# Five local edits and one order table in a fused two-block kernel on Trainium2

## The chip, the core and the metric

The kernel runs on one core of one Trainium2 chip. The metric is the device time of one execution in microseconds (us). A comparison is made between medians of runs of the two kernels on the same chip. A core has five engines that run their own instruction queues and meet at semaphores: TensorE (PE, matmuls), VectorE (DVE), ScalarE (ACT), GpSimd (POOL) and SyncE (SP, which here only issues DMAs).

## The reference, cut to what matters

The input is one sequence of 512 tokens with 1024 channels. A first block adds a mixer (a bidirectional state-space branch and a windowed attention, gated and joined) and an MLP; a second block has its own mixers, a cross attention to a memory and a second MLP. The state-space branch has 8 groups of 4 heads:

```python
def rmsnorm(x, g):
    y = xf * lax.rsqrt(jnp.mean(xf * xf, axis=-1, keepdims=True) + EPS)
    return y * g
...
def ssd_branch(z, xbc, dt_raw, conv_w, conv_b, dt_bias, a_log, d_skip, norm_w, w_out):
    xbc = jax.nn.silu(depthwise_conv(xbc, conv_w, conv_b))
    xs, bs, cs = split_cols(xbc, (D_INNER, G * N, G * N))
    dt = jax.nn.softplus(dt_raw + dt_bias);  a = -jnp.exp(a_log)
    y = ssd_scan(xs, dt[0], a[0], bs, cs) + flip(ssd_scan(flip(xs), ...)) + xs * d_skip
    y = gated_rmsnorm(y, z, norm_w)          # silu(z), then a norm within each group
    return y @ w_out
...
x = x + rmsnorm(mixed, post_mix_norm);  h = rmsnorm(x, pre_mlp_norm)
f = jnp.square(jax.nn.relu(h @ w_mlp_in)) @ w_mlp_out
x = x + rmsnorm(f, post_mlp_norm)
```

The second block's mixer projects the normed x to, among others, three latents of 256, 128 and 64 columns, each with an rms norm of its own. The last MLP of the kernel is multiplied by a scheme that replaces eight block products by seven (products n = 0 to 6, sums of blocks p1, c11, c12, c21, c22).

## The kernel before, in words

All products are in fp32 made of two halves: an operand is split into a high part (hh, whi, ua_h, by ACT) and the remainder (hl, wlo, ua_l, by DVE), and three matmuls add up one product: lines L286 to L288 with 512 moving columns, L304 to L306 with 256. Weights come in tiles of 128x1024 (raw); L140 casts one to whi on ACT and L141 takes the rest, wlo, on DVE. Tiles in PSUM are eight banks, named after their users (psg, pse, psc, pso, psy, pst).

The program is written in source order with Python lists of steps; a scheduling layer then fixes the order on each engine. `issue_after(x)` holds instructions back until x has been issued, `keep_in_program_order` keeps one in its place. On an engine instructions run strictly in that order.

*Start.* x comes in four tiles of 128 tokens. For each, ACT squares one half and DVE the other, two short DVE instructions form the mean, POOL takes the power -0.5, and DVE and ACT scale one half each (L417, L418) before PE transposes. The bias dtb and alog are loaded 4 bytes per partition on SP's queue, behind the weights of bc0; dtb is first used by dt_evac (L486), alog by L490. gpre (L400) is the first norm's gain, transposed by PE.

*State-space groups.* `Group` is one of 8 groups; a group takes some 52 us. A loop runs a list of steps, GSEQ, which mixes the second half of group g with the preparation of group g+1: z0 to z3 are the projections of z for the current group, f0 to f7 the projections and convolutions of the next group's channels (psg evacuated by L591 to cbuf and L592, four taps on DVE at L594, silu at L595), xt0 and xt1 the transposes of its two tiles of x (L600, copied by L601), st, w and y the states, weights and outputs (L667 with xw of L664, L697, L705), norm the group's norm (squares L724, the power on POOL at L343, scaling of sz at L729), u0 and u1 the transposes of the normed result (L734, split by L337 and L338 into ua_h and ua_l), e0 to e3 the exponents of the decay (PE L685, Exp L687 on ACT, masking L688 and sum L692 on POOL), cb the product of C and B (L656). rows loads rh and lh for the exponents on POOL's queue. silu and Exp need different tables on ACT, so a change between them costs an ACT_TABLE_LOAD. In the fifth group the f steps also carry half of the output projection.

*After a block's output.* `post_norm` works in eight tiles k: pn and the sum into xT (L1027, L1028), the split into hh and hl (L337, L338), and the squares of the new x for the next norm, by `SumSq`: a square on ACT (L1008) and an add into ssq on POOL (L1009). It runs twice: in front of the first block's MLP (PE L1045 to L1047) and in front of the second block's mixer (`project`, PE L1248 to L1250). `token_sums` sums ssq over channels with a product by ones on PE (L349).

*Latents.* `inv_rms` takes mean and power of one latent's four columns (L342, L343), three times.

*Last quarter.* Products n = 0 to 6 run over two row halves i. What is ready is copied and added into the blocks (L1804, `add`, L1784) by the table LAST, and DONE says which is stored after which product. Each of the products has a bank of PSUM for each half.

Of the kernel before, what the change touches and what calls it, by code (L numbers as in the profile page):

```python
# [16 lines left out]
P = 128  # L17
# [11 lines left out]
GSEQ = """  # L29
z0 w0 xt1 st0 z1 w1 z2 z3 st1 silu st2 y0 f0 f1 y1 rows f2 f3 w2 e0 y2 e1 w3 f4 f5 bt y3 norm f6 e2 xt0 f7 u0 u1 cb e3  # L30
"""
# [53 lines left out]
def body(ctx, tc, a, out, dbg=None):  # L85
# [318 lines left out]
    for t in range(NT):  # L404
        for i in range(2):
            xs = xn[:, t, i * 512 : i * 512 + 512]
            junk = sb("cacc", bufs=3)
            if i == 0:
                A.activation(junk, xs, AF.Square, accum_out=ss0[:, t, i : i + 1])
            else:  # L410
                V.tensor_tensor_reduce(out=junk, in0=xs, in1=xs, scale=1.0, scalar=0.0, op0=ALU.mult, op1=ALU.add,
                                       accum_out=ss0[:, t, i : i + 1])
        rt = r0[:, t : t + 1]
        V.tensor_tensor(out=rt, in0=ss0[:, t, 0:1], in1=ss0[:, t, 1:2], op=ALU.add)
        V.tensor_scalar(out=rt, in0=rt, scalar1=1.0 / D, scalar2=EPS, op0=ALU.mult, op1=ALU.add)
        last = tc.keep_in_program_order(G.tensor_tensor(out=rt, in0=rt, in1=mhalf[:, 0:1], op=ALU.pow))
        V.tensor_scalar(out=xn[:, t, 0:512], in0=xn[:, t, 0:512], scalar1=rt, scalar2=None, op0=ALU.mult)  # L417
        A.activation(xn[:, t, 512:1024], xn[:, t, 512:1024], AF.Copy, scale=rt)  # L418
        for k in range(KT):
# [42 lines left out]

    dtb = const([P, 1], "dtb")
    alog = const([P, 1], "alog")
    with tc.issue_after(unit_of["bc", 0].last.ins):
        with nc.allow_non_contiguous_dma(reason="128 scalars"):
            for hf in range(2):
                nc.sync.dma_start(out=dtb[64 * hf : 64 * hf + 64, :], in_=a["dt_bias"].rearrange("o d h -> (d h) o"))
                nc.sync.dma_start(out=alog[64 * hf : 64 * hf + 64, :], in_=a["a_log"].rearrange("o d h -> (d h) o"))
        load_params()  # L470
        dskip = small(const([P, 32], "dskip"), a["d_skip"])
# [523 lines left out]
    class SumSq:  # L995
# [20 lines left out]
    def post_norm(gain, ssq, next_gain, side):  # L1016
# [779 lines left out]
    def gather(n, i, po, q):  # L1796
# [24 lines left out]
    def second(q, w):  # L1821
        raws = (w[0, 0], w["t3"], w[1, 0], w[1, 0], w[0, 0], w[0, 1], w[1, 1])
        for n in range(7):
# [13 lines left out]
            for i in range(2):  # L1837
# [61 lines left out]
```

## Time and profile before

| | |
|---|---|
| median of 3 runs | 1914.93 us (1913.95 to 1914.96) |
| profiled execution, device time | 1915.58 us |
| its span in the profile | 1913.8 us |
| mean granted TensorE clock | 0.994 |
| busy share PE, DVE, ACT, POOL | 96%, 60%, 49%, 23% |

An engine's busy time counts its running instructions only. A wait of PE is read with what released it; the granted clock of a stretch is 1.00 at 2.4 GHz and 0.50 at 1.2 GHz. Timeline rows give start and duration in us, with the engine's idle time before the row and its releaser in brackets.

### The profile page before, as it was taken

The page shows a single profiled execution, that of the slowest core. Times are in us where ns is not written, and L with a number is a line of the kernel's source. Part 1 is how long each engine was busy: PE and PEld are TensorE (multiplying, and loading weights), DVE is VectorE, ACT ScalarE, POOL GpSimd, SP SyncE. Part 2 cuts the span into 40 slices and gives each one's busy share as a digit, 9 for nine tenths or more (in the row PEclk, how much of TensorE's full clock was granted, in tenths as well). Part 3 has the DMA queues.
Part 4 walks back from the last instruction along what each step waited for, and adds up shares of the span by engine and source line. Part 5 has one row for each costly group of instructions (what it writes and reads, how often), then busy time and mean ns, then how long its engine had stood idle before and what let it go on. Part 6 is the DMA issues. An engine that isn't in the chain of part 4 may idle for free. (4 is left out here: it accounts for less than half of the span.)

```text
span 1913.8 us, 24517 instructions
## 1 busy us (share of the span) xinstructions
PE 1846.5 (96%) x9585; PEld 1525.0 (80%) x9585; DVE 1142.9 (60%) x1796; ACT 937.4 (49%) x1511; POOL 439.4 (23%) x498
## 2 busy tenths in 40 slices
PE   8899999999999999998999999989999999999998
PEld 7688888888887777887888888878877768888886
DVE  6767762666456554537233434567667785766768
ACT  6756672766335665345332313345443454444534
POOL 1454441443202321234011201231210330000000
PEclk9999999999999999999999999999999999999999
DMA  5222112221332222333333232322211232324211
GB/s 170 75 68 68 52 62 88 68 68 46 102 93 66 82 79 67 126 119 110 100 98 111 88 110 89 110 74 59 73 45 55 78 132 77 125 85 132 88 44 44
DMA packets 161186, 164.10 MB, mean 86 GB/s; under 512 B 8743, under 2 KB 148718, under 8 KB 161071
## 3 DMA queue, kind: packets, MB, share of 16 engines
q1 hardware_dynamic: 148858, 150.90, 25.0%
q10 hardware_dynamic: 9716, 10.02, 1.7%
q0 software_dynamic: 2496, 1.61, 0.4%
q8 instruction: 75, 1.23, 0.3%
q14 instruction: 41, 0.33, 0.1%
HBM read 158.26 MB, written 4.23 MB: 85 GB/s over the span
## 5 line engine op out<-in xcount | busy, mean ns | idle before, releaser
L141 DVE TENSOR_TENSOR wlo<-raw,whi 128x1024 fp32r<-128x1024 f32 (+3 forms) x253 | 321.4, 1286 | 223.5 <-ACT whi L140 219.3
L286 PE MATMUL psg<-hh,whi 128*128 128x512 f32 (+1 forms) x1016 | 404.2, 398 | 0.8 <-DVE hl L338 0.8
L287 PE MATMUL psg<-hl,whi 128*128 128x512 f32 (+1 forms) x1016 | 401.0, 395 | 0.0
L140 ACT CAST whi<-raw 128x1024 fp32r<-128x1024 f32 (+3 forms) x253 | 254.7, 1028 | 298.4 <-PE psg L287 255.0
L288 PE MATMUL psg<-hh,wlo 128*128 128x512 f32 (+1 forms) x1016 | 399.5, 393 | 0.0
L286 PEld LDWEIGHTS psg<-hh,whi 128*128 128x128 f32 (+1 forms) x1016 | 191.0, 188 | 40.3 <-issue 1.2
L288 PEld LDWEIGHTS psg<-hh,wlo 128*128 128x128 f32 (+1 forms) x1016 | 191.0, 188 | 39.8
L287 PEld LDWEIGHTS psg<-hl,whi 128*128 128x128 f32 (+1 forms) x1016 | 190.9, 188 | 38.2 <-DVE hl L335 0.4
L286 PE MATMUL psg<-ua_h,whi 128*128 128x512 f32 x544 | 216.3, 399 | 0.8 <-DVE xT L1585 0.5
L287 PE MATMUL psg<-ua_l,whi 128*128 128x512 f32 x544 | 213.8, 393 | 0.0
L288 PE MATMUL psg<-ua_h,wlo 128*128 128x512 f32 x544 | 212.7, 391 | 0.0
L304 PE MATMUL psg<-whi,hh 128*128 128x256 f32 x416 | 122.1, 294 | 10.1 <-ACT cacc L592 3.6
L286 PEld LDWEIGHTS psg<-ua_h,whi 128*128 128x128 f32 x544 | 102.0, 188 | 26.0 <-DVE xT L1585 2.4
L305 PE MATMUL psg<-wlo,hh 128*128 128x256 f32 x416 | 119.8, 288 | 1.0 <-DVE wlo L141 1.0
L306 PE MATMUL psg<-whi,hl 128*128 128x256 f32 x416 | 120.2, 289 | 0.0
L287 PEld LDWEIGHTS psg<-ua_l,whi 128*128 128x128 f32 x544 | 102.3, 188 | 21.7 <-issue 1.0
L288 PEld LDWEIGHTS psg<-ua_h,wlo 128*128 128x128 f32 x544 | 102.2, 188 | 20.8
L1187 POOL TENSOR_TENSOR fsq<-relu 128x512 f32<-128x512 f32 x32 | 40.5, 1267 | 243.5 <-ACT relu L1184 228.2
L1009 POOL TENSOR_TENSOR ssq<-ssq,sq 128x512 f32<-128x512 f32 x42 | 66.3, 1578 | 117.2 <-ACT sq L1008 115.9
L141 DVE TENSOR_TENSOR wlo<-quad,whi 128x1024 fp32r<-128x1024 f32 x56 | 66.9, 1222 | 43.0 <-ACT whi L140 43.0
L304 PEld LDWEIGHTS psg<-whi,hh 128*128 128x128 f32 x416 | 80.0, 192 | 15.7 <-ACT sz L630 5.1
L140 ACT CAST whi<-quad 128x1024 fp32r<-128x1024 f32 x56 | 57.0, 1049 | 70.0 <-PE psg L287 32.9
(628 smaller groups left out, 3547.7 us busy)
## 6 DMA issues: line engine op xcount, KB each, us to landing
raw<-in_w_in_dram SPq DMA_DIRECT2D x37, 1024.0 KB
raw<-in_w_mlp_in_dram SPq DMA_DIRECT2D x16, 1024.0 KB
raw<-in_w_mlp_out_dram SPq DMA_DIRECT2D x16, 1024.0 KB
raw<-in_w_ff_dram SPq DMA_DIRECT2D x16, 1024.0 KB
quad<-in_w_ff_dram SPq DMA_DIRECT2D x16, 1024.0 KB
raw<-in_w_in_dram SPq DMA_DIRECT2D x16, 512.0 KB
raw<-in_w_ssd_out_dram SPq DMA_DIRECT2D x8, 1024.0 KB
raw<-in_w_attn_out_dram SPq DMA_DIRECT2D x4, 1024.0 KB
```

The lines of the kernel that those rows point to most:

```text
L140: A.copy(self.hi[sl], self.raw[sl])
L141: V.tensor_tensor(out=self.lo[sl], in0=self.raw[sl], in1=self.hi[sl].bitcast(F32), op=ALU.subtract)
L286: T.matmul(o, lhsT=u.hi[:, k, c:e], rhs=xh[k], start=k == 0, stop=False)
L287: T.matmul(o, lhsT=u.hi[:, k, c:e], rhs=xl[k], start=False, stop=False)
L288: T.matmul(o, lhsT=u.lo[:, k, c:e], rhs=xh[k], start=False, stop=k == u.kt - 1)
L304: T.matmul(o, lhsT=xh[k][:, tk], rhs=u.hi[:, k, 0 : u.n], start=k == 0, stop=False)
L305: T.matmul(o, lhsT=xh[k][:, tk], rhs=u.lo[:, k, 0 : u.n], start=False, stop=False)
L306: T.matmul(o, lhsT=xl[k][:, tk], rhs=u.hi[:, k, 0 : u.n], start=False, stop=k == u.kt - 1)
L1009: G.tensor_tensor(out=self.t, in0=self.t, in1=q, op=ALU.add)
L1187: G.tensor_tensor(out=f, in0=r, in1=r, op=ALU.mult)
```

## The change

Six edits. The order table:

```diff
-... bt y3 norm f6 e2 xt0 f7 u0 u1 cb e3
+... bt y3 norm f6 f7 xt0 u0 e2 u1 cb e3
```

The bias transfer moves from SP's queue (behind bc0's weights) to POOL's queue at the start, and the first norm forms all four tiles' powers before any scaling, the last tile's second half being scaled on DVE:

```diff
+    dtb = const([P, 1], "dtb")
+    alog = const([P, 1], "alog")
+            G.dma_start(out=dtb[64 * hf : 64 * hf + 64, :], in_=a["dt_bias"].rearrange("o d h -> (d h) o"))
+            G.dma_start(out=alog[64 * hf : 64 * hf + 64, :], in_=a["a_log"].rearrange("o d h -> (d h) o"))
...
-                A.activation(junk, xs, AF.Square, accum_out=ss0[:, t, i : i + 1])
+                counted = A.activation(junk, xs, AF.Square, accum_out=ss0[:, t, i : i + 1])
...
         last = tc.keep_in_program_order(G.tensor_tensor(out=rt, in0=rt, in1=mhalf[:, 0:1], op=ALU.pow))
+    for t in range(NT):
+        rt = r0[:, t : t + 1]
         V.tensor_scalar(out=xn[:, t, 0:512], in0=xn[:, t, 0:512], scalar1=rt, scalar2=None, op0=ALU.mult)
-        A.activation(xn[:, t, 512:1024], xn[:, t, 512:1024], AF.Copy, scale=rt)
+        if t < NT - 1:
+            with tc.issue_after(counted.ins):
+                A.activation(xn[:, t, 512:1024], xn[:, t, 512:1024], AF.Copy, scale=rt)
+        else:
+            V.tensor_scalar(out=xn[:, t, 512:1024], in0=xn[:, t, 512:1024], scalar1=rt, scalar2=None, op0=ALU.mult)
```

In post_norm the squares come behind the last tile, with their adds on DVE:

```diff
-            split_from(xT[:, k, :], hh[:, k, :], hl[:, k, :], pcol(next_gain + k))
-            nsq.add(xT[:, k, :])
+            ins = A.activation(hh[:, k, :], xT[:, k, :], AF.Copy, scale=pcol(next_gain + k))
+            V.scalar_tensor_tensor(out=hl[:, k, :], in0=xT[:, k, :], scalar=pcol(next_gain + k), in1=hh[:, k, :].bitcast(F32),
+                                   op0=ALU.mult, op1=ALU.subtract)
+        with tc.issue_after(ins.ins):
+            for k in range(KT):
+                nsq.add(xT[:, k, :], V)
```

The three powers of the latents become one of 12 columns, and in the last quarter two sums go another way (c21 and c22 no longer take product 0 and product 1 in two adds; product 1 is added to p1 on its way out of PSUM), with other banks for the products 4 and 5:

```diff
-        inv_rms(lat[:, i, :], lat[:, i, :], n, NT)
+        V.tensor_scalar(out=lat[:, i, :], in0=lat[:, i, :], scalar1=1.0 / n, scalar2=EPS, op0=ALU.mult, op1=ALU.add)
+    G.tensor_tensor(out=rates, in0=rates, in1=mhalf[:, 0 : 3 * NT], op=ALU.pow)
...
-        if n < 2:
+        if n == 0:
             A.copy(block(name, i), pv4)
+        elif n == 1:
+            V.tensor_tensor(out=block(name, i), in0=pv4, in1=block("p1", i), op=ALU.add)
...
-    LAST = {0: ("c11", "c12", "c21", "c22"), 1: ("c21", "c22"), ...
+    LAST = {0: ("c11", "c12"), 1: ("c21", "c22"), ...
...
-                    o = bank("e" if q == 3 and n == 5 else "g")
+                    o = bank({4: "co"[i], 5: "e"}.get(n, "g") if q == 3 else "g")
```

What the order table does on the engines is seen at the end of the third group (about 209 us in the profile before). On ACT, of the kernel before, behind the last square of the group's norm; cacc of L595 is the tile of f6, e the two exponents, sz the group's output before the transposes:

```order
L724 ACTIVATE xd_1927,ssg_1722<-sz_1555 128x256
L687 ACT_TABLE_LOAD
L687 ACTIVATE e_318_1954<-pse_1952 128x512
L595 ACT_TABLE_LOAD
L595 ACTIVATE cacc_1900<-cacc_1900,pv 128x512
L729 ACTIVATE sz_1555<-sz_1555,ssg_1722 128x256 x4
L687 ACT_TABLE_LOAD
L687 ACTIVATE e_320_1959<-pse_1957 128x512
L601 COPY xt_1964<-pst_1965 128x4x128
L591 COPY cbuf_1984<-psg_1939 128x512
L592 ACTIVATE cacc_1983<-psg_1939,pv 128x512
```

And of the changed kernel, whose lines stand 6 further on in this part (L595 is L601, L729 is L735, L687 is L693):

```order
L730 ACTIVATE xd_1927,ssg_1722<-sz_1555 128x256
L735 ACTIVATE sz_1555<-sz_1555,ssg_1722 128x256 x2
L601 ACTIVATE cacc_1900<-cacc_1900,pv 128x512
L735 ACTIVATE sz_1555<-sz_1555,ssg_1722 128x256 x2
L597 COPY cbuf_1965<-psg_1939 128x512
L598 ACTIVATE cacc_1964<-psg_1939,pv 128x512
L607 COPY xt_1975<-pst_1976 128x4x128
L337 ACTIVATE ua_h<-pso_1982,pv 128x512
L693 ACT_TABLE_LOAD
L693 ACTIVATE e_323_1991<-pse_1989 128x512
```

The silu of f6's tile stands behind two of the four scalings of sz, no table is loaded before it, and the evacuation of f7 (cbuf, cacc) comes before the exponents, which were ahead of it.

On PE, in the kernel before, from the last two matmuls of f7; pst with cacc are the transposes xt0, pso and psy with sz u0 and u1, psc is cb, psg_2036 the first tile of z:

```order
L287 MATMUL psg_1939<-hl,whi_1724 128x512
L288 MATMUL psg_1939<-hh,wlo_1725 128x512
L656 MATMUL psc_2008<-cT_1557,bT_1556 128x128 x4
L685 MATMUL pse_2013<-rh_30_266,lh_28_264 128x512
L304 MATMUL psg_2036<-whi_1866,hh 128x256
L305 MATMUL psg_2036<-wlo_1867,hh 128x256
L306 MATMUL psg_2036<-whi_1866,hl 128x256
L600 MATMUL pst_1965<-ident,cacc_1900 128x128 x4
L734 MATMUL pso_1994<-ident,sz_1555 128x128
```

And of the changed kernel:

```order
L287 MATMUL psg_1939<-hl,whi_1724 128x512
L288 MATMUL psg_1939<-hh,wlo_1725 128x512
L606 MATMUL pst_1976<-ident,cacc_1900 128x128 x4
L740 MATMUL pso_1982<-ident,sz_1555 128x128 x4
L691 MATMUL pse_1989<-rh_30_266,lh_28_264 128x512
L691 MATMUL pse_1994<-rh_31_267,lh_29_265 128x512
L740 MATMUL psy_2001<-ident,sz_1555 128x128 x4
L662 MATMUL psc_2008<-cT_1557,bT_1556 128x128 x4
L304 MATMUL psg_2036<-whi_1866,hh 128x256
```

xt0 and u0 follow f7 directly; cb, one exponent and three matmuls of z stood in front of them and stand behind them now.

On DVE, at the end of post_norm's loop in front of the second block's mixer; pn and xT are the loop's sum, ssq the squares. Before:

```order
L1027 SCALAR_TENSOR_TENSOR pn_9944<-acc,pv,pst_9824 128x512
L338 SCALAR_TENSOR_TENSOR hl<-xT,pv,hh 128x512
L1028 TENSOR_TENSOR xT<-xT,pn_9936 128x512
L1028 TENSOR_TENSOR xT<-xT,pn_9944 128x512
L141 TENSOR_TENSOR wlo_9960<-raw_9835,whi_9959 128x8x128
L338 SCALAR_TENSOR_TENSOR hl<-xT,pv,hh 128x512
L141 TENSOR_TENSOR wlo_9960<-raw_9835,whi_9959 128x8x72
L338 SCALAR_TENSOR_TENSOR hl<-xT,pv,hh 128x512
L1282 TENSOR_REDUCE sel_f_10196<-ident 128x4
L342 TENSOR_SCALAR rtok_1549_9957<-pst_10106 128x4
L141 TENSOR_TENSOR wlo_10288<-raw_9965,whi_10287 128x8x128
L1348 TENSOR_TENSOR lf_10274<-pj_9958,b_if_10189 128x32
```

And of the changed kernel (L1028 is L1034, L338 is L1036, L1009 is L1015, L141 keeps its number):

```order
L1034 TENSOR_TENSOR xT<-xT,pn_9920 128x512
L1034 TENSOR_TENSOR xT<-xT,pn_9925 128x512
L141 TENSOR_TENSOR wlo_9960<-raw_9835,whi_9959 128x8x128
L1036 SCALAR_TENSOR_TENSOR hl<-xT,pv,hh 128x512 x2
L1015 TENSOR_TENSOR ssq_9889<-ssq_9889,sq_9931 128x512
L141 TENSOR_TENSOR wlo_9960<-raw_9835,whi_9959 128x8x72
L1015 TENSOR_TENSOR ssq_9889<-ssq_9889,sq_9934 128x512
L1292 TENSOR_REDUCE sel_f_10196<-ident 128x4
L1015 TENSOR_TENSOR ssq_9889<-ssq_9889,sq_9937 128x512
L141 TENSOR_TENSOR wlo_10286<-raw_9965,whi_10285 128x8x128
```

The adds into ssq, which POOL did, stand on DVE between the splits of the weights.

## Rows read from the trace of the kernel before

**Rows 1.** The page's first part: busy us, share of the span, instructions.

```profile
PE 1846.5 (96%) x9585; PEld 1525.0 (80%) x9585; DVE 1142.9 (60%) x1796; ACT 937.4 (49%) x1511; POOL 439.4 (23%) x498
```

**Rows 2.** Waits of PE over the whole span, by its line and the releaser: total us, times, longest us.

```profile
PE pst L600 <- ACT cacc L595: 8.0, 11, 1.2
PE psg L1249 <- DVE hl L338: 5.7, 5, 1.6
PE psg L304 <- ACT cacc L592: 3.6, 6, 0.7
```

**Rows 3.** Busy time by stretch in the first group, with the granted clock (PEclk): two stretches in which PE stood, and the one behind each. Columns: stretch, length, busy us (instructions) of PE, PEld, DVE, ACT, POOL, then PEclk, DMA share, GB/s.

```profile
75.00:78.00 3.00, 0.12 (x1) 0.13 (x2) 3.00 (x5) 0.45 (x2) 3.00 (x5) 1.00 0.57 150
78.80:82.10 3.30, 3.11 (x8) 1.92 (x8) 3.30 (x5) 0.58 (x1) 2.29 (x3) 0.50 0.51 124
88.00:91.80 3.80, 1.74 (x9) 1.16 (x7) 1.35 (x3) 3.56 (x4) 3.25 (x6) 1.00 0.00 0
92.50:95.80 3.30, 3.30 (x11) 2.73 (x11) 2.46 (x5) 3.03 (x5) 2.34 (x3) 0.50 0.00 0
```

**Rows 4.** The start: timelines of ACT and PE at dt's evacuation, the stretch behind it (columns as in rows 3), and two rows of DVE's timeline in the first norm.

```profile
23.62 0.95 ACT L486 ACTIVATE acc<-psg,dtb 64x256 f32<-64x256 f32 x2 [1.62 <-DMA dtb<-in_dt_bias_dram]
24.62 0.58 PE L304 MATMUL psg<-whi,hh 128*128 128x256 f32 x1 [3.36 <-ACT acc L486]
24.70:27.40 2.70, 2.70 (x13) 2.70 (x14) 2.65 (x4) 1.77 (x4) 0.00 (x0) 0.50 0.05 14
7.90 1.04 DVE L417 TENSOR_SCALAR acc<-acc,r 128x512 f32<-128x512 f32 x2
10.11 0.17 DVE L400 COPY gpre<-pst 128x8 f32<-128x8 f32 x1 [1.17 <-PE pst L398]
```

**Rows 5.** post_norm: durations (ns, min/median/max) of hl and of the sum into xT over the kernel; then the first MLP's entry as a stretch (columns as in rows 3) and DVE's groups in it (count | busy us, mean ns | idle before).

```profile
L338 DVE SCALAR_TENSOR_TENSOR hl<-xT,pv,hh x32: 740/929/1780, 868.1 to 1575.3; 128x512 fp32r<-128x512 f32 x32
L1028 DVE TENSOR_TENSOR xT<-xT,pn x16: 677/687/1771, 866.3 to 1254.5; 128x512 f32<-128x512 f32 x16
868.20:897.60 29.40, 24.55 (x98) 17.42 (x97) 26.73 (x29) 15.79 (x26) 16.16 (x10) 1.00 0.22 68
L338 DVE SCALAR_TENSOR_TENSOR hl<-xT,pv,hh 128x512 fp32r<-128x512 f32 x8 | 7.9, 983 | 0.0
L1028 DVE TENSOR_TENSOR xT<-xT,pn 128x512 f32<-128x512 f32 x6 | 6.1, 1046 | 0.0
L141 DVE TENSOR_TENSOR wlo<-raw,whi 128x1024 fp32r<-128x1024 f32 x4 | 6.0, 1492 | 0.9 <-ACT whi L140 0.9
```

**Rows 6.** The mixer's entry: the stretch and a part of it (columns as in rows 3), and DVE's groups in it.

```profile
1240.80:1275.60 34.80, 28.19 (x203) 26.76 (x202) 23.69 (x30) 16.48 (x30) 13.40 (x15) 0.90 0.25 76
1259.80:1266.50 6.70, 6.68 (x31) 6.68 (x32) 0.75 (x2) 0.00 (x0) 0.19 (x1) 0.50 0.20 51
L338 DVE SCALAR_TENSOR_TENSOR hl<-xT,pv,hh 128x512 fp32r<-128x512 f32 x8 | 9.2, 1153 | 0.0
L1028 DVE TENSOR_TENSOR xT<-xT,pn 128x512 f32<-128x512 f32 x8 | 6.5, 832 | 0.0
L141 DVE TENSOR_TENSOR wlo<-raw,whi 128x576 fp32r<-128x576 f32 x1 | 1.8, 1835 | 0.0
```

**Rows 7.** Powers on POOL (L343): durations in ns for the latents (4 columns) and for 8 columns; and PE's row at the latents' transposes.

```profile
L343 POOL TENSOR_TENSOR lat<-lat,mhalf x3: 1001/1176/1321, 1279.9 to 1282.2; 128x4 f32<-128x4 f32 x3
L343 POOL TENSOR_TENSOR krs<-krs,mhalf x1: 1647/1647/1647, 889.5 to 889.5; 128x8 f32<-128x8 f32 x1
1282.65 0.63 PE L1319 MATMUL pst<-ident,pj 128*128 128x128 f32 x4 [1.55 <-DVE pj L1332]
```

**Rows 8.** The last quarter as a stretch (columns as in rows 3).

```profile
1868.90:1906.00 37.10, 32.74 (x141) 25.83 (x141) 36.93 (x47) 20.33 (x24) 0.00 (x0) 1.00 0.10 30
```

**Rows 9.** ACT's timeline at the end of the third group (start us, duration us).

```profile
209.04 1.28 ACT L687 ACT_TABLE_LOAD   x1
210.94 1.28 ACT L595 ACT_TABLE_LOAD   x1
212.24 0.72 ACT L595 ACTIVATE cacc<-cacc,pv 128x512 f32<-128x512 f32 x1
212.87 1.69 ACT L729 ACTIVATE sz<-sz,ssg 128x256 f32<-128x256 f32 x4
221.86 0.71 ACT L630 COPY sz<-psg 128x256 f32<-128x256 f32 x2
```

**Rows 10.** The same place: POOL's power, PE's timeline, and a DMA issue of POOL (count, KB each, us to landing).

```profile
209.30 1.48 POOL L343 TENSOR_TENSOR ssg<-ssg,mhalf 128x4 f32<-128x4 f32 x1 [2.76 <-DVE ssg L342]
209.84 0.39 PE L288 MATMUL psg<-hh,wlo 128*128 128x512 f32 x1
210.07 1.05 PE L656 MATMUL psc<-cT,bT 128*128 128x128 f32 x8
213.01 0.66 PE L600 MATMUL pst<-ident,cacc 128*128 128x128 f32 x4 [1.19 <-ACT cacc L595]
222.35 0.39 PE L304 MATMUL psg<-whi,hh 128*128 128x256 f32 x1 [0.39 <-ACT sz L630]
228.48 0.70 PE L667 MATMUL pso<-xw,bt 128*128 128x256 f32 x2 [0.46 <-DVE xw L664]
rh<-csd POOLq DMA_DIRECT2D x2, 16.0 KB, 2.0
```

More of the change, by code (lines that the diff above doesn't have):

```diff
@@ L29 @@
 GSEQ = """
-z0 w0 xt1 st0 z1 w1 z2 z3 st1 silu st2 y0 f0 f1 y1 rows f2 f3 w2 e0 y2 e1 w3 f4 f5 bt y3 norm f6 e2 xt0 f7 u0 u1 cb e3
+z0 w0 xt1 st0 z1 w1 z2 z3 st1 silu st2 y0 f0 f1 y1 rows f2 f3 w2 e0 y2 e1 w3 f4 f5 bt y3 norm f6 f7 xt0 u0 e2 u1 cb e3
 """
@@ L389, in body @@
     unit_of["z", 0].load()
+    dtb = const([P, 1], "dtb")
+    alog = const([P, 1], "alog")
+    with nc.allow_non_contiguous_dma(reason="128 scalars"):
+        for hf in range(2):
+            G.dma_start(out=dtb[64 * hf : 64 * hf + 64, :], in_=a["dt_bias"].rearrange("o d h -> (d h) o"))
+            G.dma_start(out=alog[64 * hf : 64 * hf + 64, :], in_=a["a_log"].rearrange("o d h -> (d h) o"))
     V.memset(ones, 1.0)
@@ L460, in small @@
         return t
-    dtb = const([P, 1], "dtb")
-    alog = const([P, 1], "alog")
     with tc.issue_after(unit_of["bc", 0].last.ins):
[L466 to L469, printed above, removed]
         load_params()
@@ L1000, in __init__, with add @@
             self.first = True
-        def add(self, src):
+        def add(self, src, eng=None):
             if self.first:
@@ L1008, in add @@
                 A.activation(q, src, AF.Square)
-                G.tensor_tensor(out=self.t, in0=self.t, in1=q, op=ALU.add)
+                (eng or G).tensor_tensor(out=self.t, in0=self.t, in1=q, op=ALU.add)
         def rms(self):
@@ L1329, in body @@
     for i, n in enumerate((256, 128, 64)):
-        inv_rms(lat[:, i, :], lat[:, i, :], n, NT)
+        V.tensor_scalar(out=lat[:, i, :], in0=lat[:, i, :], scalar1=1.0 / n, scalar2=EPS, op0=ALU.mult, op1=ALU.add)
+    rates = lat.rearrange("p i t -> p (i t)")[:, 0 : 3 * NT]
+    G.tensor_tensor(out=rates, in0=rates, in1=mhalf[:, 0 : 3 * NT], op=ALU.pow)
     for i, (c0, n) in enumerate(((8, 256), (264, 128), (392, 64))):
@@ L1808, in gather @@
             store(DONE[n], i)
-    LAST = {0: ("c11", "c12", "c21", "c22"), 1: ("c21", "c22"), 2: ("c11",), 3: ("c21",), 4: ("c21", "c22", "c12"), 5: ("c22", "c12"), 6: ("c12",)}
+    LAST = {0: ("c11", "c12"), 1: ("c21", "c22"), 2: ("c11",), 3: ("c21",), 4: ("c21", "c22", "c12"), 5: ("c22", "c12"), 6: ("c12",)}
     DONE = {2: "c11", 4: "c21", 5: "c22", 6: "c12"}
```

## The prediction

> **What bounds the kernel now.** I read the page's busy shares first, then what TensorE (PE) waits for, then the stretches in which its clock was low, and last the engines' own sequences around each edit. PE is busy 96% of the span [rows 1], so an edit pays only by shortening one of its waits or a stretch at half clock; the 60% of VectorE (DVE) and the 49% of ScalarE (ACT) matter only where PE waits for them. The longest lists of waits [rows 2] lie where the change works: the silu of a state-space group's first tile of x (L595), the conv's evacuation (L592), the entry of the mixer (L338 before L1249).
>
> The clock comes second. After PE stood still in 75 to 78 us, and again in 88 to 91.8 us, the next 3.3 us ran at a granted clock of 0.50, which is 1.2 GHz instead of 2.4 [rows 3]. The same follows the 3.36 us wait at 21 us [rows 4] and the chain of waits in the mixer's entry [rows 6].
>
> **The change part by part.** The sum is made against the profiled execution, 1915.58 us; the median of the runs is 0.65 below it.
>
> *Bias transfer.* L486 stood 1.62 us for dt_bias, and PE 3.36 us for L486 [rows 4]. On POOL's queue at the start the bytes land long before 22 us: -1.6. The 1.7 us left of PE's wait may still be followed by half clock; if not, half of the 2.7 us at 0.50 comes back too (1.35). The cover that could go: the Exp of a_log is now sixth in ACT's order, ahead of the squares of x's last two tiles. POOL's loads at a group's end land 2.0 us after issue [rows 10], and four issues go one behind the other, so a_log is due at about 5 to 7 us, about when ACT, which squares beside DVE, would start the third tile's square, shortly before DVE's scales at 7.90 [rows 4]. I take no stall, and 2 us as the worst.
>
> *First norm.* Today DVE scales tiles 0 and 1 at 7.90 to 8.94, ahead of the copy of gpre that waits for PE until 10.11 [rows 4]. In the new order all scales stand behind the sums, so these 1.04 us, which lay under that wait, go onto the path. The last tile's second half, which ACT did, adds 0.49 on DVE, and taking the tiles in one run returns about 0.8 that DVE waited for POOL: +0.75 (bounds 0 and +1).
>
> *Norm squares.* In the first MLP's entry, 96 of the 98 matmuls at 0.23 us each (two neighbours of [rows 10] start 0.23 apart) are 22.1 us of the 29.4 [rows 5]: 7.3 are lost. While POOL adds beside them, hl averages 0.983 there and xT 1.046; the shortest of each in the kernel are 0.74 and 0.68 [rows 5]. Undone, that is 8 x 0.24 + 6 x 0.37 = 4.1 us, and wlo, slowed beside them too, is put at 1 more; DVE's groups show 0.9 us of idle time in 29.4. I take -5.0 (bounds -4, and -7 for all that is lost). In the mixer's entry the same arithmetic gives 8 x 0.41 + 8 x 0.15 = 4.5, and 1.0 more for the wlo of 576 columns at 1.84; PE idles 6.6 there, and 6.7 us ran at 0.50, a loss of 3.35 [rows 6]. Against that stands a wait that is new: PE's token sums now follow seven adds on DVE, 0.68 each with two wlo between, about 7.3 us behind the last hl, 2.3 us after PE gets there. 5.5 + 3.35 - 2.3, less about half of a stretch that the new wait may bring back (0.9): -5.6; I take -5.5 (bounds -4.0 and -6.6).
>
> *One power.* A power takes 1.00 us on 4 columns and 1.65 on 8 [rows 7], 0.16 a column, so 12 take about 2.3, an estimate beyond the rows' sizes. The first result comes 1.0 later than after 1.32, PE's 1.55 us wait grows by it, and a smaller wait behind loses 0.3: +0.7 (bounds 0 and +1).
>
> *Last quarter.* Two adds fewer for DVE, and banks that free the fourth product earlier. DVE is busy 36.93 of 37.10 us there [rows 8], so what PE gains at one wait it meets again at the next; two adds at 0.69, less about 1 us in which DVE now waits for a cast or a copy: -0.3 (bounds -1.5 and 0).
>
> *The order at a group's end,* seven times. The example is the group that ends at 210 us. Three steps.
>
> First, PE. Today, behind the 24 matmuls of f7, PE does cb, an exponent and three matmuls of z before it waits 1.19 us for the silu, which ends at 212.96 [rows 9, 10]. In the new order nothing stands between f7 and the transposes of that silu's tile, and without the two exponents inside f7 PE is there at 209.8. On ACT the silu has moved behind the first two scalings of sz (L729), and these wait for the power on POOL, which ends at 210.78 [rows 10]. Two scalings are 0.8, so the silu runs from 211.6 to 212.35: PE stands 2.6 us instead of 1.19, and work of 1.5 us that lay in front of the wait now lies behind it.
>
> Second, ACT. From 209.04 to the copies of z at 221.86 it runs without a pause today, 12.82 us with three table loads, of which [rows 9] shows two. The new order has the same instructions and three table loads, but waits until 210.78 for POOL (1.74), and f7's own silu (0.63 to the next instruction) has come in front of the copies: 12.82 + 1.74 + 0.63 = 15.19, the copy at 224.23. The third tile of z needs its bank and starts 0.49 behind the copy, as today at 222.35 [rows 10]: 224.72, which is 2.4 later, with 0.45 of transposes already done: 1.9. The xw wait behind it, 0.46 at 228.48 [rows 10], partly goes: 1.6 late.
>
> Third, the clock. A stand of 2.6 us is like those of [rows 3], and half clock over 3.4 us costs 1.7; ACT's lateness hides about 0.3: 1.4. So 3.0 a boundary with the stretch, 1.6 without. The Trainium skill, "TensorE: Matmul & The Clock Gate", section "Part 1: The HAM clock gate (the 'warmup' mystery)", says that the throttled clock is the default and that activity releases it. By that rule the change comes out at the +8.5 below, and without it at +0.1. The trace agrees in both stands of [rows 3].
>
> At six ends ACT waits for the power in this way; at the fifth, near 359 us, the power is long done and only the second step holds, 1.5. Sum: 6 x 3.0 + 1.5 = 19.5 (bounds: 7 x 0.4 = 3 where only the first wait grows and two others go, and 28 with a second stretch at each of the six).
>
> Other places: -1.6 + 0.75 - 5.0 - 5.5 + 0.7 - 0.3 = -10.95. **Sum: +8.5, 1924.1 profiled, 1923 in the runs.**
>
> **Rivals.**
> - *The order is nearly free; faster.* The evacuation of f7 now follows the silu closely, so the waits for L592 (0.6) and L630 (0.39) could go, against 1.4 more at the silu: +0.4 an end, 1915.6 - 10.95 + 3 - 0.65 = 1907. It decides if the copy of z comes no later than today; below 1.0 us an end the kernel is measurably faster. For it: the two waits are there today [rows 2, 10]. Against it: ACT has no pause there to give.
> - *The clock holds.* 6 x 1.6 + 1.5 - 10.95 = +0.1: 1915. For it: the other work around each stand is dense, and no stand of 2.6 us at this place exists in the trace. Against it: [rows 3].
> - *a_log holds up the first norm,* up to +2, with the stretches: 1925; and a second stretch at each end, 1932.
>
> **How the numbers follow.** A difference under about 0.2% (3.8 us) can't be told from none. Forecast and what lies above it 0.53; the clock holds, or holds at most ends, 0.22; the order nearly free 0.25. Slower 0.53, same 0.22, faster 0.25. The range takes in the free order's lower part but for a tenth, and the second stretches: 1904 to 1932. The forecast's own range is 1919 to 1932.
>
> **What would show it.** Right: in the profile after, PE waits for the silu's transposes over 2 us at six ends, with a window at 0.50 behind; ACT idles for POOL's power just before; the third tile of z starts about 2 us later than today measured from the last matmul of f7; the first MLP's entry takes 24 to 25 us, the mixer's 29 to 30 with a new wait at the token sums; ACT no longer waits for dtb. Wrong: the silu's wait stays near 1.2, or the granted clock stays at 1.00 over the groups, or the entries keep their length because squares on ACT, not adds, set DVE's pace.

## The result, and the profile after

The changed kernel takes 1941.14 us (median of 4 runs, 1938.93 to 1944.96) against 1914.95 (1913.95 to 1916.41): 1.0134 times as long, with a 95% interval of 1.0116 to 1.0152. That is 26 us slower where the forecast said 8 slower, and lies above the range. The profiled execution took 1942.88 us, 27.3 more than the profiled one of before.

The page's first part of the changed kernel, to be read against [rows 1]:

```profile
PE 1860.1 (96%) x9585; PEld 1540.3 (79%) x9585; DVE 1140.7 (59%) x1809; ACT 931.9 (48%) x1504; POOL 421.9 (22%) x486
```

PE executes as many instructions, 9585, and is busy 13.6 us longer, which fits its longer time at half clock (64.7 us against 20.4, in the table below); the other half of the loss is in waits. The main waits of PE after the change (line and releaser, total us, times, longest us; L601 and L606 are L595 and L600 of before, L691 is L685, L673 is L667, L636 is L630, L1015 is L1009, L1329 is L1319; L432 with L425 are the first transposes, L420 with L417):

```profile
PE pst L606 <- ACT cacc L601: 16.9, 7, 3.9
PE pse L691 <- DMA lh<-gld: 9.2, 9, 1.5
PE pso L673 <- DVE xw L670: 4.3, 5, 1.7
PE psg L432 <- DVE acc L425: 3.8, 1, 3.8
PE pst L349 <- DVE ssq L1015: 2.7, 1, 2.7
PE psg L304 <- ACT sz L636: 2.6, 1, 2.6
PE pst L1329 <- DVE pj L1344: 2.3, 1, 2.3
PE psg L304 <- ACT acc L492: 1.6, 1, 1.6
```

The wait for the first silu has doubled (8.0 in [rows 2], 16.9 now), and a wait of 9.2 us has appeared that was next to nothing: exponents that wait for the load of lh, which POOL issues late (at the third end first at 234.04, 13.3 us behind the sum of the group's last square; before, 3.6 behind it). The wait for hl at the mixer (5.7 in [rows 2]) has left this list, the token sums' new one (2.7) is in it.

To see where the time went I took, for PE's n-th matmul, its start in the changed kernel less its start in the kernel before; both execute equally many matmuls, in places in another order. How much this difference grows from place to place, and how much of each stretch the changed kernel spent at a granted clock of 0.50 (worked out from the two traces; before it was 10.2 us in the start, 6.8 in the mixer's entry, 3.4 in the rest and none elsewhere):

```
place (time before, us)    growth   at 0.50    forecast
start, to 100               +0.5      6.8        -0.85
first end, 100-145          +7.6     10.2        +3.0
second, 145-197             +3.9      6.8        +3.0
third, 197-250              +3.1      6.8        +3.0
fourth, 250-320             +2.7      3.4        +3.0
fifth, 320-398              +2.3      0          +1.5
sixth, 398-450              +4.4      6.8        +3.0
seventh, 450-518            +4.1      3.4        +3.0
518-860                     +2.0      0           0
first MLP's entry           -4.9      0          -5.0
mixer's entry, latents      +2.1     13.7        -4.8
rest                         0.0      6.8        -0.3
sum                        +27.7                 +8.5
```

Four places make the miss of 19.2 us: the ends (28.1 for 19.5), the mixer's entry (2.1 for -4.8), 518 to 860 us (2.0 for 0) and the start, where -0.85 was due. The 2.0 are in the main two waits of PE, 0.94 and 0.83 us, for loads of xk. The kernel below with dt_bias alone moved has a wait of 1.40 there and the one called "the silu first" has none, so no edit can be held to account for them.

The third end of the changed kernel is the place of [rows 9, 10]. ACT's timeline (start us, duration us, then in brackets its idle time before and what ended it):

```profile
220.77 0.19 ACT L730 ACTIVATION_READ_ACCUMULATOR xd<-sz 128x1 f32 x1
222.75 0.91 ACT L735 ACTIVATE sz<-sz,ssg 128x256 f32<-128x256 f32 x2 [1.79 <-POOL ssg L343]
223.57 0.70 ACT L601 ACTIVATE cacc<-cacc,pv 128x512 f32<-128x512 f32 x1
...
230.69 0.60 ACT L693 ACTIVATE e<-pse 128x512 f32<-128x512 f32 x1 [0.54 <-PE pse L691]
231.31 1.28 ACT L601 ACT_TABLE_LOAD   x1
232.61 0.73 ACT L601 ACTIVATE cacc<-cacc,pv 128x512 f32<-128x512 f32 x1
233.35 1.28 ACT L693 ACT_TABLE_LOAD   x1
...
237.02 0.37 ACT L636 COPY sz<-psg 128x256 f32<-128x256 f32 x1
```

PE's waits at the same end, and the granted clock (PEclk, the column behind POOL's) in four stretches around them:

```profile
224.32 1.12 PE L606 MATMUL pst<-ident,cacc 128*128 128x128 f32 x4 [2.61 <-ACT cacc L601]
236.38 0.47 PE L691 MATMUL pse<-rh,lh 128*128 128x512 f32 x1 [1.23 <-DMA lh<-gld]
237.47 0.77 PE L691 MATMUL pse<-rh,lh 128*128 128x512 f32 x1 [0.62 <-ACT sz L636]
```

```profile
221.70:224.40 2.70, 0.09 (x2) 0.08 (x2) 0.12 (x1) 1.65 (x4) 1.11 (x3) 0.87 0.11 35
223.80:227.00 3.20, 2.67 (x11) 2.38 (x12) 0.81 (x2) 3.20 (x7) 0.00 (x0) 0.50 0.00 0
235.00:237.40 2.40, 0.63 (x3) 0.19 (x1) 1.19 (x1) 2.40 (x5) 2.32 (x6) 0.99 0.13 21
237.50:240.70 3.20, 3.20 (x14) 3.10 (x15) 3.20 (x3) 1.75 (x4) 3.20 (x3) 0.50 0.00 0
```

ACT idles 1.79 us for POOL's power, PE stands 2.61 us for the silu, and the second silu with a table load on either side (231.31 to 234.63) runs ahead of the copy of z at 237.02. From the end of the square's sum to that copy it is now 16.06 us (220.96 to 237.02), against 12.82 before and 15.19 forecast. PE stands a second time beside it, and a stretch at half clock begins at the end of each stand.

### The profile page after: what moved, and what is told of

Read it like the earlier page. It is cut to its first block, busy times and chain, and to the rows that moved or that the text cites. A ratio compares the mean times of both kernels' runs of the same rounds, so it can differ in the third digit from the quotient of the medians.

```text
span 1941.2 us, 24474 instructions
## 1 busy us (share of the span) xinstructions
PE 1860.1 (96%) x9585; PEld 1540.3 (79%) x9585; DVE 1140.7 (59%) x1809; ACT 931.9 (48%) x1504; POOL 421.9 (22%) x486
## 3 DMA queue, kind: packets, MB, share of 16 engines
q0 software_dynamic: 2624, 1.61, 0.4%
## 4 chain that ended last, share of the span: by engine, by line
PE 58%; DVE 7%; issue 3%; POOL 1%; ACT 1%; DMA 1%; ACTq 0%; DVEq 0%; POOLq 0%
PE psg L286 13%; PE psg L287 13%; PE psg L288 13%; DVE wlo L141 2%; PE psg L1864 1%; PE psg L1863 1%; PE psg L1862 1%; PE pse L887 1%; PE psg L305 1%; PE psg L304 1%; PE psg L306 1%; POOL rs L343 1%; PE psy L935 1%; PE pst L925 1%; DMA xk<-in_x_dram 1%
## 5 line engine op out<-in xcount | busy, mean ns | idle before, releaser
L141 DVE TENSOR_TENSOR wlo<-raw,whi 128x1024 fp32r<-128x1024 f32 (+3 forms) x253 | 324.8, 1301 | 238.4 <-ACT whi L140 234.3
L141 DVE TENSOR_TENSOR wlo<-quad,whi 128x1024 fp32r<-128x1024 f32 x56 | 66.9, 1222 | 44.1 <-ACT whi L140 44.1
L305 PEld LDWEIGHTS psg<-wlo,hh 128*128 128x128 f32 x416 | 82.8, 199 | 2.9 <-DVE wlo L141 1.2
```

The costliest lines, as they stand in the source:

```text
L141: V.tensor_tensor(out=self.lo[sl], in0=self.raw[sl], in1=self.hi[sl].bitcast(F32), op=ALU.subtract)
L305: T.matmul(o, lhsT=xh[k][:, tk], rhs=u.lo[:, k, 0 : u.n], start=False, stop=False)
```

## The experiments

Each ratio is to the kernel before on the same chip, with its 95% interval. "Growth" is the measure of the table above.

**The order alone.** The kernel before with one changed line of the order table:

```diff
-... bt y3 norm f6 e2 xt0 f7 u0 u1 cb e3
+... bt y3 norm f6 f7 xt0 u0 e2 u1 cb e3
```

> The kernel before with the new order of steps at the state-space groups' ends and nothing else. Counted by PE's matmuls, the changed kernel falls 28 us behind between 100 and 500 us, so theory A (the order alone makes the loss) expects 1915 + 26 to 30, 1941 to 1945, with waits of 2.6 us for the silu (L595) at six ends and a stretch at 0.50 behind nearly all of them. Theory B (a part of the loss comes from the five other edits, which shift the first group and the weights' arrival) expects what the forecast gave the order, 1915 + 19.5 = 1934 or less.

1941.0 us, ratio 1.0125 (1.0109 to 1.0141). The order alone makes nearly all of the loss, and its seven ends grow by 5.2, 3.2, 2.8, 2.8, 2.3, 4.3 and 3.4 us, 23.9 together.

**The five places alone.** The changed kernel with the old line of the table:

```diff
-... bt y3 norm f6 f7 xt0 u0 e2 u1 cb e3
+... bt y3 norm f6 e2 xt0 f7 u0 u1 cb e3
```

> The changed kernel with the old order at the groups' ends: the five other edits alone. The offsets of the changed kernel outside the groups (start +1.7, wait for xk +2.0, first MLP's entry -4.9, mixer's entry +1.7, latents +0.4, last quarter -0.3) add up to +0.6: theory A expects 1914 to 1917. The forecast's sum for the same edits was -10.95: theory B, that they keep it when the groups run as before, expects 1904 to 1906.

1913.32 us, ratio 0.9984 (0.9974 to 0.9994): together they give 3 us, not 11.

**Each place by itself.** The bias transfer alone:

```diff
+    dtb = const([P, 1], "dtb")
+    alog = const([P, 1], "alog")
+    with nc.allow_non_contiguous_dma(reason="128 scalars"):
+        for hf in range(2):
+            G.dma_start(out=dtb[64 * hf : 64 * hf + 64, :], in_=a["dt_bias"].rearrange("o d h -> (d h) o"))
+            G.dma_start(out=alog[64 * hf : 64 * hf + 64, :], in_=a["a_log"].rearrange("o d h -> (d h) o"))
```

> The kernel before with the bias transfer moved to POOL's queue and nothing else; the Exp of a_log stands sixth on ACT. In the changed kernel a_log landed at 10.1 us and ACT stood for it from 6.9. Theory A (the transfer hurts more at the front than it saves at L486): PE's first matmul of dt 2 to 4 us late, no wait for dtb at L486, and some 3 to 4 us lost in the first group, as with the five edits together (offset +4.3 at 120 us): 1917 to 1920. Theory B (the forecast's): -1.6 at L486 and no stall, 1913 to 1914.

1918.35 us, ratio 1.0012 (1.0001 to 1.0023), as theory A had it. PE's wait for L486 falls from 3.36 to 1.64 us, but PE stands 4.26 us before the first transposes, while ACT waits 3.74 us for a_log ahead of x's third square; and the first end grows by 3.3 us. The first norm alone:

```diff
+    for t in range(NT):
+        rt = r0[:, t : t + 1]
         V.tensor_scalar(out=xn[:, t, 0:512], in0=xn[:, t, 0:512], scalar1=rt, scalar2=None, op0=ALU.mult)
-        A.activation(xn[:, t, 512:1024], xn[:, t, 512:1024], AF.Copy, scale=rt)
+        if t < NT - 1:
+            with tc.issue_after(counted.ins):
+                A.activation(xn[:, t, 512:1024], xn[:, t, 512:1024], AF.Copy, scale=rt)
+        else:
+            V.tensor_scalar(out=xn[:, t, 512:1024], in0=xn[:, t, 512:1024], scalar1=rt, scalar2=None, op0=ALU.mult)
```

> The kernel before with the first norm's new order and nothing else; x's squares don't wait for a_log here. The forecast's step: scales no longer hidden under the wait for gpre, first matmul of dt 0.75 us later, nothing else: 1915 to 1916.5. If it also changes the first group (offset at 120 us above 2), the loss there isn't the bias transfer's.

1917.53 us, ratio 1.0003 (0.9993 to 1.0014): no change, as forecast. The norm squares alone:

```diff
-            split_from(xT[:, k, :], hh[:, k, :], hl[:, k, :], pcol(next_gain + k))
-            nsq.add(xT[:, k, :])
+            ins = A.activation(hh[:, k, :], xT[:, k, :], AF.Copy, scale=pcol(next_gain + k))
+            V.scalar_tensor_tensor(out=hl[:, k, :], in0=xT[:, k, :], scalar=pcol(next_gain + k), in1=hh[:, k, :].bitcast(F32),
+                                   op0=ALU.mult, op1=ALU.subtract)
+        with tc.issue_after(ins.ins):
+            for k in range(KT):
+                nsq.add(xT[:, k, :], V)
```

> The kernel before with the squares behind the last tile and their adds on DVE, both calls, and nothing else. The forecast gave -5.0 for the first MLP's entry and -5.5 for the mixer's: 1904.5. With all five edits and the old order the offsets were -5.0 and -2.6 (two stretches at 0.50 behind a wait of 2.74 us at the token sums): 1907 to 1908.5. In the changed kernel the mixer's entry lost 1.7; if that belongs to the edit, 1911 to 1912.

1907.9 us, ratio 0.9963 (0.9948 to 0.9978): 7 us, the best of the parts. The first MLP's entry gives 4.96 of it.

**Only dt_bias on POOL's queue,** a_log left on SP's, where it was:

```diff
+            G.dma_start(out=dtb[64 * hf : 64 * hf + 64, :], in_=a["dt_bias"].rearrange("o d h -> (d h) o"))
...
-                nc.sync.dma_start(out=dtb[64 * hf : 64 * hf + 64, :], in_=a["dt_bias"].rearrange("o d h -> (d h) o"))
```

> The kernel before with dt_bias on POOL's queue but a_log left on SP's, so that no Exp waits ahead of the first norm's squares. Theory A (a_log's landing at 10.1 us makes the bias transfer's loss at the start): first matmul of dt within 0.5 us of before, no wait of L486 for dtb, 1913 to 1915. Theory B (the loss of e7 at the first group's end, 3.3 us, comes from what else moves with the transfer, the rows of parameters earlier on SP): it shows here too, offset 3 at 145 us, 1916 to 1918.

1920.76 us, ratio 1.0022 (1.0012 to 1.0031): not better than with a_log beside it. That doesn't clear the Exp of a_log. PE's stand before the first transposes falls from 4.26 to 2.16 us, but the Exp now waits for a_log just ahead of dt's evacuation, and PE's wait for that evacuation is 2.94 us instead of 1.64. What both kernels share is the growth of the first end, 4.0 us here and 3.3 there. ACT's timeline of this kernel at the third and fourth square of x's tiles, and at the Exp:

```profile
8.99 0.63 ACT L414 ACTIVATE cacc<-acc 128x512 f32<-128x512 f32 x1 [2.34 <-DMA acc<-in_x_dram]
...
10.58 0.63 ACT L414 ACTIVATE cacc<-acc 128x512 f32<-128x512 f32 x1 [0.86 <-DMA acc<-in_x_dram]
...
24.61 0.20 ACT L492 ACTIVATE na<-alog 128x1 f32<-128x1 f32 x1 [1.66 <-DMA alog<-in_a_log_dram]
```

And 4 to 8 us as a stretch (columns as in [rows 3], the last is GB/s), in the kernel before and in this one:

```profile
4.00:8.00 4.00, 4.00 (x25) 4.00 (x24) 2.54 (x11) 2.10 (x7) 0.84 (x2) 1.00 1.02 403
```

```profile
4.00:8.00 4.00, 4.00 (x30) 4.00 (x29) 1.82 (x8) 1.45 (x4) 0.84 (x2) 1.00 0.76 278
```

With the 4-byte rows of dt_bias under way, 278 GB/s move instead of 403, and the third tile of x itself lands later: its square starts at 8.99 instead of 7.35, the fourth at 10.58 instead of 9.20. In all four kernels with such transfers 278 to 318 GB/s move in this stretch, in the others 399 to 410.

**The silu first.** The new order, but the scalings of sz are issued behind the first silu, so that it need not wait for POOL's power:

```diff
+        def scale(self, nx=None):
+            with tc.issue_after(nx.silus[0].ins) if nx else ExitStack():
+                for c in range(NT):
+                    A.activation(self.sz[:, c, :], self.sz[:, c, :], AF.Copy, scale=self.ss[:, c : c + 1])
```

> The order of e1, but ACT issues the four scalings of sz (L729 in before) only behind the silu of f6's tile, so that the silu doesn't stand behind POOL's power. If the silu's place behind the power makes the long stand of PE and the stretch at 0.50 behind it, PE's wait for L595 falls from 2.6 to about 0.9 at six ends, the stretches behind these waits go, and of the order's loss of about 28 some 12 to 20 us come back: 1922 to 1930. If what costs is the rest of ACT's sequence (two exponents and a second silu ahead of the copies of z), the wait falls but no more than 5 us come back: 1937 to 1940.

1940.76 us, ratio 1.0123 (1.0107 to 1.0140); the profiled execution, 1932.8, is its shortest. Its ACT timeline at the third end:

```profile
214.27 0.19 ACT L725 ACTIVATION_READ_ACCUMULATOR xd<-sz 128x1 f32 x1
215.35 0.72 ACT L595 ACTIVATE cacc<-cacc,pv 128x512 f32<-128x512 f32 x1 [0.89 <-DVE cacc L594]
...
229.26 0.38 ACT L631 COPY sz<-psg 128x256 f32<-128x256 f32 x1
```

The power is out of the silu's way and PE waits for it 0.91 us instead of 2.61; yet the copy of z still comes 15.0 us behind the square, and the second to fourth ends grow by 2.15 to 2.2 instead of 2.8 to 3.2. The wait that I took for the first cause is the smaller part of the price.

**Work for PE in the stand.** Ten unread matmuls ahead of the silu's transposes at six ends, to hold the clock:

```diff
+                for _ in range(fill):
+                    T.matmul(pt, lhsT=hh[:, 0, 0:P], rhs=hh[:, 0, :], start=True, stop=True)
```

> The order of e1, with ten matmuls of 128x512 that nobody reads in front of the transposes xt0 at six ends: 2.3 us of extra work for PE, in the time in which it would stand 2.6 us. No wait gets shorter. If the half clock behind the stand is a cost of its own, the granted clock stays at 1.00 behind these six places and each end gains 1 to 1.5 us: 6 to 9 us less than e1. If the half clock there is hidden by ACT's lateness, the time is that of e1 within 2 us. If the ten matmuls delay PE, it is up to 5 us above.

1949.34 us, ratio 1.0163 (1.0148 to 1.0178), 8 us above the order alone, where 5 was the most expected. Inconclusive: at the third end, behind the filling, PE still waited 1.73 us for the silu, the scheduler put ACT's exponents elsewhere, and a new wait of 2.48 us for one of them came in.

**f7 early, the rest as before:**

```diff
-... bt y3 norm f6 e2 xt0 f7 u0 u1 cb e3
+... bt y3 norm f6 f7 e2 xt0 u0 u1 cb e3
```

> The kernel before with half of the new order: f7 is moved ahead of xt0, but the exponents e2 stay ahead of xt0 (f6 f7 e2 xt0 u0 u1 cb e3). On ACT the silu of f6's tile still stands between the scalings behind POOL's power, and the second silu with its two table loads still stands ahead of the copies of z, so the arithmetic of the forecast gives the copy of z at the same 224.2 us of the example and PE's wait for the silu at 2.1 instead of 2.6. Theory A (f7's place and what ACT does for it makes the loss): 1915 + 18 to 26. Theory B (the loss comes from the exponents e2 being late, through the loads of rh and lh behind them): 1915 + 0 to 6.

1936.4 us, ratio 1.0114 (1.0097 to 1.0132). Of the reordering, f7 in front of xt0 makes the larger part: 20 of 25 us.

**The second silu late.** As the kernel with the silu first, but the silu of f7 is issued behind the first copy of z:

```diff
+            elif self.g:
+                with tc.issue_after(self.zc.ins):
+                    silu(2 * self.g + j, self.xs[j])
```

> The order of e3 (new steps, first silu ahead of the scalings), and in addition ACT issues the silu of f7's tile only behind the copy of z, together with the transposes xt1 that need it. That takes the second silu and two table loads (0.63 and 2 x 1.28 = 3.2 us of ACT) out of the stretch between the group's norm and the copy of z. Theory A (ACT's sequence up to the copy of z sets PE's loss at each end): e3 and e5 lost 2.2 to 2.4 an end at five ends, here at most 0.5, so 1915 + 0 to 6. Theory B (what remains is the PE order itself, or the exponents behind the loads of rh and lh): still 2 an end, 1915 + 14 or more.

1915.11 us, ratio 0.9985 (0.9972 to 0.9997): the whole loss of the order is gone. ACT at the third end:

```profile
208.84 0.19 ACT L734 ACTIVATION_READ_ACCUMULATOR xd<-sz 128x1 f32 x1
209.92 0.72 ACT L598 ACTIVATE cacc<-cacc,pv 128x512 f32<-128x512 f32 x1 [0.89 <-DVE cacc L594]
...
220.50 0.37 ACT L637 COPY sz<-psg 128x256 f32<-128x256 f32 x1
220.88 1.28 ACT L598 ACT_TABLE_LOAD   x1
222.17 0.72 ACT L598 ACTIVATE cacc<-cacc,pv 128x512 f32<-128x512 f32 x1
```

The second silu and its table load now stand behind the copy of z, which comes 11.7 us after the square. The loads of lh are late here too, the first issued 9.2 us behind the square's sum, and PE waits for none of them at this end. All of PE's waits at the fourth end, in the kernel before, in the order alone, and in this kernel:

```profile
265.27 0.66 PE L600 MATMUL pst<-ident,cacc 128*128 128x128 f32 x4 [1.19 <-ACT cacc L595]
270.32 0.39 PE L304 MATMUL psg<-whi,hh 128*128 128x256 f32 x1 [0.58 <-ACT cacc L592]
274.61 0.39 PE L304 MATMUL psg<-whi,hh 128*128 128x256 f32 x1 [0.51 <-ACT sz L630]
278.42 0.65 PE L600 MATMUL pst<-ident,cacc 128*128 128x128 f32 x4 [0.21 <-ACT cacc L595]
280.73 1.45 PE L667 MATMUL pso<-xw,bt 128*128 128x256 f32 x4 [0.47 <-DVE xw L664]
```

```profile
277.51 0.66 PE L600 MATMUL pst<-ident,cacc 128*128 128x128 f32 x4 [2.61 <-ACT cacc L595]
288.61 0.47 PE L685 MATMUL pse<-rh,lh 128*128 128x512 f32 x1 [1.21 <-DMA lh<-gld]
289.65 0.47 PE L685 MATMUL pse<-rh,lh 128*128 128x512 f32 x1 [0.57 <-ACT whi L140]
293.40 1.47 PE L667 MATMUL pso<-xw,bt 128*128 128x256 f32 x4 [1.61 <-DVE xw L664]
```

```profile
261.98 0.66 PE L603 MATMUL pst<-ident,cacc 128*128 128x128 f32 x4 [2.17 <-ACT cacc L598]
```

The brackets add up to 2.96, 6.00 and 2.17 us. The last kernel stands at the silu nearly as long as the order alone does and loses nothing, since no other wait follows: five waits have become one. The order alone has three more behind the silu, 3.04 us over the kernel before, and grew by 2.78 at this end without any half clock.

**What pays.** The squares (as above) and the last quarter on the kernel before:

```diff
-        if n < 2:
+        if n == 0:
             A.copy(block(name, i), pv4)
+        elif n == 1:
+            V.tensor_tensor(out=block(name, i), in0=pv4, in1=block("p1", i), op=ALU.add)
...
-                    o = bank("e" if q == 3 and n == 5 else "g")
+                    o = bank({4: "co"[i], 5: "e"}.get(n, "g") if q == 3 else "g")
```

> The kernel before with the norm squares' edit and the last quarter's edit, old order, nothing else. e9 gave 1907.9 for the squares; the offset over the last quarter was -0.3 in the changed kernel and in the one with the five edits: 1907 to 1908. If the last quarter's edit saved its two adds on the path: 1906.

1909.71 us, ratio 0.9956 (0.9943 to 0.9970). And both edits on the kernel with the second silu late:

> e10's order together with the two edits of e11. If the parts add up: e10's time less 8. With theory A of e10: 1907 to 1913.

1907.04 us, ratio 0.9949 (0.9930 to 0.9968): faster than both kernels of the case. It isn't told apart from the one without the order, whose interval overlaps.

## Why the prediction was wrong

Three terms failed. The order's second step charged 1.6 us an end for the late copy of z, which came 3.2 us late and cost about that; the cover of the bias transfer was put at nothing and cost more than the transfer saved; and 3.35 us of half clock in the mixer's entry were counted as the change's to win, which they weren't.

**The order's mechanism held; its weights didn't.** PE's stand of 2.6 us, ACT's idle 1.79 us for the power (1.74 forecast), the late copy of z and the half clock are there as the three steps had them. But the prediction hung the argument on the first step, the silu behind the power. The runs put the price on the second. Third end, from the start of the square's last row on ACT to the copy of z, and the growth of that end, in one profiled execution of each kernel:

```
kernel                 square to copy, us   less before   growth
second silu late             11.66             -1.37        -0.97
before                       13.03              0            0
silu first                   14.99             +1.96        +2.20
f7 early                     15.59             +2.56        +2.45
order alone                  15.60             +2.57        +2.81
changed kernel               16.25             +3.22        +3.13
```

Here, and at the second and fourth ends of these kernels, the growth follows the lateness of the copy within 0.4 us, whatever PE waits for first. At the other ends it departs from it by up to 2.0. I had worked this sequence out as 2.37 late and then took 0.8 of it away, for transposes already done and for the xw wait; it was 3.2 late and 0.1 came off. Part of the missing 0.85 shows: ACT waits 0.54 us for an exponent that PE takes up only at 230.26, among the matmuls of z. The xw wait, which was to go in part, is gone at this end but not everywhere: at the fourth end of the order alone it is 1.61 where it was 0.47.

**The clock.** A stretch was put at 1.4 us on top of the waits. In the order alone, the second to fourth ends spent 6.8, 3.4 and 0 us at half clock and grew by 3.2, 2.8 and 2.8. A stretch is thus paid mostly out of waits: where PE runs slowly it waits less for ACT (its waits at these ends add up to 4.7, 4.6 and 6.0). At the fourth end PE stood 2.61 us, and both stretches behind it ran at full clock:

```profile
277.50:280.90 3.40, 3.39 (x28) 3.21 (x29) 1.53 (x3) 3.38 (x7) 0.00 (x0) 1.00 0.00 0
280.90:288.00 7.10, 6.50 (x50) 5.94 (x49) 4.57 (x7) 7.03 (x10) 5.50 (x11) 1.00 0.03 4
```

So the two errors, 1.6 for ACT and 1.4 for the clock, cancelled by luck at the second to fourth ends: 3.0 forecast, 2.7 to 3.9 measured. The rival with a second stretch at each end priced the order at 28, and 28.1 is what it came to, but not by that mechanism: two stretches apart came at the second, third and sixth ends, and the order alone makes 23.9 of it, the other edits 4.2.

**The ends that aren't like the third.** One end was taken as the pattern of six. The first grew by 7.6 (5.2 with the order alone), the last two by 4.4 and 4.1, the fifth by 2.3 for 1.5. At the first, the changed kernel grows by 2.4 more than the order alone. The bias transfer goes with such a growth: +3.3 with it alone and +4.0 with dt_bias alone, against 0 to +1.3 in kernels with neither it nor the new order. But these edits also change the order of the first group on the engines. With the transfer alone, 171 of PE's matmuls up to 113 us are others than those at the same place of the kernel before, and on ACT the silu of f6's tile, which ran ahead of the group's last square, runs behind it. The kernel before, and the bias transfer alone:

```profile
106.99 0.72 ACT L595 ACTIVATE cacc<-cacc,pv 128x512 f32<-128x512 f32 x1 [0.34 <-DVE cacc L594]
107.93 0.19 ACT L724 ACTIVATION_READ_ACCUMULATOR xd<-sz 128x1 f32 x1
...
117.89 0.69 ACT L630 COPY sz<-psg 128x256 f32<-128x256 f32 x2
```

```profile
109.50 0.19 ACT L724 ACTIVATION_READ_ACCUMULATOR xd<-sz 128x1 f32 x1
...
112.91 0.72 ACT L595 ACTIVATE cacc<-cacc,pv 128x512 f32<-128x512 f32 x1
...
122.54 0.71 ACT L630 COPY sz<-psg 128x256 f32<-128x256 f32 x2
```

From the square's last row to the copy of z it was 9.96 us and is 13.04, as at the third end, and 3.1 more is close to the growth of 3.3. So the price there is more likely that of another order than of bytes moved 100 us earlier. No run holds the old order with the transfer moved, so this isn't shown, nor why the scheduling layer chose the new one. Why the last two ends cost more wasn't tried.

**Bias.** The wait of L486 for dt_bias is gone and PE's 3.36 us is 1.6, as forecast. The step that failed is the cover: a_log was due at 5 to 7 us and landed at 10.1, where ACT in the changed kernel stood for it:

```profile
10.19 0.20 ACT L496 ACTIVATE na<-alog 128x1 f32<-128x1 f32 x1 [3.31 <-DMA alog<-in_a_log_dram]
```

The x tiles, which the prediction didn't count among what the transfers meet, landed late as well, as the kernel with dt_bias alone shows. PE then stood 3.77 us before the first transposes. In the changed kernel the start took half a us more instead of 0.85 less, within the spread there (starts that nothing had changed came out 2.4 us earlier to 2.5 later).

**Norm squares.** The first MLP's entry is the part that came out within 0.1 us, and by the mechanism forecast: hl takes 0.749 us for 0.983, the sum into xT 0.688 for 1.046 (the same stretch and groups as in [rows 5]):

```profile
898.80:923.26 24.46, 23.26 (x99) 17.65 (x98) 22.91 (x33) 15.20 (x23) 3.13 (x2) 1.00 0.25 80
L1036 DVE SCALAR_TENSOR_TENSOR hl<-xT,pv,hh 128x512 fp32r<-128x512 f32 x8 | 5.7, 749 | 0.0
L1034 DVE TENSOR_TENSOR xT<-xT,pn 128x512 f32<-128x512 f32 x6 | 4.0, 688 | 0.0
```

The mixer's entry did not. The new wait for the token sums is there (2.74, forecast 2.3), and the waits for hl have fallen from 5.7 to 0.8. Up to the token sums PE's waits add up to 4.0 us instead of 6.5, so the forecast's 5.5 less 2.3 came out at 2.5. But the 3.35 us counted as regained from the clock were not in the change's gift. Growth at this place, sorted by the time at half clock:

```
at 0.50, us    mixer as before             with the squares moved
 3.4           -1.6, -2.1, -3.2, -3.2      -4.6
 6.8            0, -0.7, -0.7              -2.2
10.2                                       -0.6, -0.4
13.7           +3.6                        +2.1
```

Even kernels whose mixer is untouched spent anything from 3.4 to 13.7 us at half clock there and moved by 7 us. At equal clock the squares give about 2: 2.1 in the first line (against the mean), and 1.7 and 1.5 in the lines of 6.8 and 13.7, where the latents' later power (+0.8) is in the right column. The profiled execution of the changed kernel happened to be one of the two with the most half clock. The step that failed is the 3.35: it took one profile's half clock for a property of the place.

**The rest.** First norm (0 for +0.75), one power (PE's wait at the latents is 2.34 for 1.55 of [rows 7], +0.8 for +0.7) and last quarter (-0.3 in the changed kernel, -0.6 beside the squares) fell as forecast.

## What to carry to other kernels

When a unit of work is moved earlier on one engine, follow what it drags along on the engine that serves it: f7 brought its own silu and two table loads ahead of the copy that frees PE's bank, and the lateness of that copy, not PE's longest wait, was most of the price. Add up all waits of a stretch before and after: one stand of 2.2 us in place of five small ones cost nothing. A stretch at half clock in one profile isn't a gain to be had; see first whether it stays when something elsewhere is changed.

## What the hardware showed that I had not expected

Transfers of 64 rows of 4 bytes on POOL's queue at the start took 5.4 to 7.0 us from issue to landing in the changed kernel, where those of 16 KB in the groups take 2.0 [rows 10]. With dt_bias alone moved, the core's DMA carried 278 GB/s instead of 403 while they were under way, and the square of x's third tile began 1.6 us later. The Trainium skill, "DMA: Bandwidth & Descriptors", section "Why small descriptors are slow (HBM only)", names a fixed overhead for each packet. No run here measures that overhead; in the stretch above the busy share of the DMA engines fell with the rate, from 1.02 to 0.76, so most of the drop is time in which they stood idle, and why stays open.

A table load takes 1.28 us, and the silu behind it starts 0.02 us after its end (231.31, 232.61). The Trainium skill, "ScalarE: Activation LUTs", section "What ACT_TABLE_LOAD costs", puts a switch at about 2.66 us with a drain; no such drain shows here, and the measurement decides.
